# Second half of the tokens in reverse order, so that one product per tile holds the keys of both halves in a gated recurrence

## The chip, the cores and the metric

The kernel runs on one core of a Trainium2 chip. The metric is the device time of one execution in microseconds (us), lower is better. All engines of the core are used: PE (matmuls and weight loads), DVE (elementwise), ACT (activations and copies), POOL, and SP, which issues DMAs.

## The reference, cut to what matters

The reference is one residual block for 256 tokens of width 1024: a SwiGLU FFN, a mixer of two branches (a gated linear recurrence and a forgetting attention), a cross attention to a memory of 256 rows, and a second FFN. The change is in the recurrence (branch A, 8 heads, 128 key channels each) and in what has to follow it. Per head, with a forget gate f between 0 and 1 for each channel:

```
f = lb + (1 - lb) * sigmoid(f_logit);  k = 1 - f;  q = silu(q)
S_t = diag(f_t) S_{t-1} + k_t i_t^T
o_t = S_t^T q_t
```

Written out, token t reads token s <= t with the weight sum over channels of q_t k_s f_{s+1} ... f_t. In the attention (branch B) the logit of t and s has the sum of log f over the tokens after s up to t.

## The kernel before, in words

All work is on 256 tokens, kept as two halves of 128 (index b or h). Every projection is a chain of matmuls on PE: each fp32 weight tile is loaded by SP, copied into a rounded part `hi` on ACT (L126), its rest `lo` is made on DVE (L127), and three products (hi·hi, hi·lo, lo·hi) are added up in PSUM. Three pools set how far loads and copies run ahead: 4 raw tiles, 8 `hi` and 8 `lo` tiles (two chunks of four). Projections write into two PSUM buffers called `mm`; the recurrence writes into four called `acc`.

The recurrence is computed by levels (`LEVELS`, L28, and then 64 and 128; loop at L703). Level 0 is the diagonal s = t. Level m, for m = 1, 2, 4, ..., 128, joins blocks of m tokens in pairs: keys of the earlier block meet queries of the later one. By then each key in an earlier block has been multiplied by all f after it in its block, and each query by all f before it. Heads are taken in two groups of four (`recs`, one `Rec` per group). A level has three steps, each for both groups:

- `products(m)` (L584): matmuls on PE, stationary operand K, moving operand Q, all 128 channels as the contraction. For m below 32 a head and a half are cut into four stretches of 32 tokens, one for each column tile of 32 columns of the array (`tile_position=(0, 32 * k)`). Only half of the 32 keys (the earlier blocks) are of use; the queries are the 16 of the later blocks (`odd`). That is 4 heads x 2 halves x 4 stretches = 32 matmuls a group. An fp32 matmul is two PE instructions, so the trace shows 128 instructions for the two groups of a level. Level 32 has 16 matmuls a group of 32 keys and 32 queries, in two column positions; level 64 has 8, level 128 has 4.
- `grow(m)` (L610): on DVE, Q and K times the products of f of the neighbour block (L619, L620, 512 elements each, two of each a level), and the products of f for blocks twice as large (L624). Both wait until the level's matmuls have read Q and K.
- `keep(m)` (L632): the wanted entries of PSUM go into the matrix AT: for m below 32 by a masked copy on DVE into `ATd` (L636, L638), then by copies on ACT (L641, L643, L646, L649). Each group has a PSUM buffer of its own (`acc`, L587).

PE's order around this is written by hand. `after(i)` (L85) puts a block at high priority behind the i-th matmul of a log; `R_AT` (L45) says behind how many matmuls after `r0` (L652) each level comes. So the levels stand as short bursts between the matmuls of other projections: first the output gate of branch A, three chunks of 344 columns (`gf`, L655, evacuated by L662 on ACT and L663, L665 on DVE), then k_b and q_b of the attention (L689, evacuated by L697). In between come the forget logits of the attention (`forget`, L673): two transposes on PE, then DVE (L678, L679), an Exp and an Ln on ACT (L681, L682), a running sum on DVE (L684) and a DMA out by POOL. Later POOL reads the sums back, spread over all partitions (L731, L735), and masks them (L737). A scheduler orders the other engines' instructions, each engine runs its own in that order.

Of the kernel before, what the change touches and what calls it, by code (L numbers as in the profile page):

```python
# [16 lines left out]
P = 128  # L17
D = 1024
# [49 lines left out]
def block_kernel(ctx: ExitStack, tc: tile.TileContext, wts, head_in, gf_in, x_in, mem_in, memT_in, cols, rows, fbias, masks, out):  # L68
# [134 lines left out]
    masks_s = cp.tile([P, len(LEVELS), 64], I32, name="masks_s")  # L203
# [322 lines left out]

    fT, kT_, qT_ = [], [], []
    for c in range(2):
        u = chunk("f_a", c)
        f, k = m4([P, 4, T], n="f"), m4([P, 4, T], n="k")  # L530
        for j in range(2):
            js = slice(2 * j, 2 * j + 2)
            ps = proj_col2(X2, u, (2 * j, 2 * j + 1))
            f_last = V.tensor_tensor(out=f[:, js], in0=ps, in1=bc(row2, [P, 2, T], 1), op=ALU.mult).ins
            S.activation(f[:, js], f[:, js], AF.Sigmoid)
            for i in (2 * j, 2 * j + 1):
                hd = 4 * c + i
                V.tensor_scalar(out=f[:, i], in0=f[:, i], scalar1=olb[:, hd : hd + 1], scalar2=lbv[:, hd : hd + 1], op0=ALU.mult, op1=ALU.add)
        V.tensor_scalar(out=k, in0=f, scalar1=-1.0, scalar2=1.0, op0=ALU.mult, op1=ALU.add)
        fT.append(f)  # L540
        kT_.append(k)
    for c in range(2):
        u = chunk("q_a", c)
        q = m4([P, 4, T], n="q")
        for j in range(2):
            js = slice(2 * j, 2 * j + 2)
            ps = proj_col2(X2, u, (2 * j, 2 * j + 1))
            z = sp.tile([P, 2, T], F32, tag="z2", name=nm("z2"), bufs=3)
            V.tensor_tensor(out=z, in0=ps, in1=bc(row2, [P, 2, T], 1), op=ALU.mult)
            S.activation(q[:, js], z, AF.Sigmoid)  # L550
            V.tensor_tensor(out=q[:, js], in0=q[:, js], in1=z, op=ALU.mult)
        qT_.append(q)
# [4 lines left out]
    masks32 = cp.tile([P, len(LEVELS) - 1, 32], I32, name="masks32")  # L557
    with tc.issue_after(f_last):
        V.tensor_tensor(out=masks32, in0=masks_s[:, : len(LEVELS) - 1, 0:32], in1=masks_s[:, : len(LEVELS) - 1, 32:64], op=ALU.bitwise_or)

    def odd(a, m):

        return a.rearrange("p (n i m) -> p n i m", i=2, m=m)[:, :, 1] if m else a

    def odd_even(g, m):
        Qv = qT_[g].rearrange("p h t -> p (h t)").rearrange("p (a i m) -> p a i m", i=2, m=m)[:, :, 1]
        Kv = kT_[g].rearrange("p h t -> p (h t)").rearrange("p (a i m) -> p a i m", i=2, m=m)[:, :, 0]
        return Qv, Kv

    class Rec:  # L570


        def __init__(self, g):
            self.g, self.f = g, fT[g]
            self.aux = m4([P, D], n="aux")

            self.ATd = self.aux[:, 256:512]
            self.T = [self.aux[:, 512:], sp.tile([P, T], F32, tag="tq", name=nm("tq"), bufs=2)]
            G.memset(self.ATd, 0.0)
            self.AT = self.f.rearrange("p h t -> p (h t)").rearrange("p (h b t) -> p h b t", h=4, b=2)  # L580
            self.cur = self.f.rearrange("p h t -> p (h t)")
            self.li = 0

        def products(self, m):  # L584

            K, Q = kT_[self.g], qT_[self.g]
            self.ps = acc()  # L587
            if m < 32:
                w = 16 if m else 32
                for i in range(4):  # L590
                    for b in range(2):
                        for k in range(4):
                            t0, o = 128 * b + 32 * k, (i * 2 + b) * w
                            MM(self.ps[32 * k : 32 * k + 32, o : o + w], K[:, i, t0 : t0 + 32], odd(Q[:, i, t0 : t0 + 32], m), start=True, stop=True, tile_position=(0, 32 * k))
            elif m == 32:
                for i in range(4):
                    for b in range(2):
                        for c in range(2):
                            t0, o = 128 * b + 64 * c, (i * 2 + b) * 32
                            MM(self.ps[64 * c : 64 * c + 32, o : o + 32], K[:, i, t0 : t0 + 32], Q[:, i, t0 + 32 : t0 + 64], start=True, stop=True, tile_position=(0, 64 * c))  # L600
            elif m == 64:
                for i in range(4):
                    for b in range(2):
                        t0 = 128 * b
                        MM(self.ps[64 * b : 64 * b + 64, i * 64 : i * 64 + 64], K[:, i, t0 : t0 + 64], Q[:, i, t0 + 64 : t0 + 128], start=True, stop=True)
            else:
                for i in range(4):
                    MM(self.ps[:, i * P : (i + 1) * P], K[:, i, 0:128], Q[:, i, 128:256], start=True, stop=True)

        def grow(self, m):  # L610

            K, Q = kT_[self.g], qT_[self.g]
            if m == 0:
                V.tensor_tensor(out=Q, in0=Q, in1=self.f, op=ALU.mult)
                return
            n = D // (2 * m)
            Tv = self.cur[:, : 2 * n].rearrange("p (a i) -> p a i", i=2)
            Qv, Kv = odd_even(self.g, m)
            V.tensor_tensor(out=Qv, in0=Qv, in1=bc(Tv[:, :, 0], [P, n, m], 2), op=ALU.mult)  # L619
            V.tensor_tensor(out=Kv, in0=Kv, in1=bc(Tv[:, :, 1], [P, n, m], 2), op=ALU.mult)  # L620
            if m < 64:
                nxt = self.T[self.li % 2]
                self.li += 1
                V.tensor_tensor(out=nxt[:, :n], in0=Tv[:, :, 0], in1=Tv[:, :, 1], op=ALU.mult)  # L624
                self.cur = nxt
            if m == 1:

                G.memset(self.AT[64:128, :, :, 0:64], 0.0)
                G.memset(self.AT[32:64, :, :, 0:32], 0.0)
                G.memset(self.AT[96:128, :, :, 64:96], 0.0)  # L630

        def keep(self, m, li):  # L632

            ps, AT = self.ps, self.AT
            if m == 0:
                V.copy_predicated(self.ATd.rearrange("p (a t) -> p a t", t=32), bc(masks32[:, li], [P, 8, 32], 1), ps[:, :256].rearrange("p (a t) -> p a t", t=32))  # L636
            elif m < 32:
                V.copy_predicated(odd(self.ATd, m), bc(odd(masks32[:, li], m), [P, 8, 16 // m, m], 1), ps[:, :128].rearrange("p (n m) -> p n m", m=m))  # L638
            elif m == 32:
                for k in range(4):  # L640
                    S.copy(AT[32 * k : 32 * k + 32, :, :, 32 * k : 32 * k + 32], self.ATd[32 * k : 32 * k + 32].rearrange("p (h b t) -> p h b t", h=4, b=2))  # L641
                for c in range(2):
                    S.copy(AT[64 * c : 64 * c + 32, :, :, 64 * c + 32 : 64 * c + 64], ps[64 * c : 64 * c + 32, :256].rearrange("p (h b t) -> p h b t", h=4, b=2))  # L643
            elif m == 64:
                for b in range(2):
                    S.copy(AT[0:64, :, b, 64:128], ps[64 * b : 64 * b + 64, :256].rearrange("p (h t) -> p h t", h=4))  # L646
            else:
                self.A128 = self.aux[:, 512:].rearrange("p (h t) -> p h t", h=4)
                S.copy(self.A128, ps.rearrange("p (h t) -> p h t", h=4))  # L649
# [23 lines left out]
    def forget(m):  # L673
# [10 lines left out]
        V.tensor_tensor_scan(out=cc, data0=ones[0:8, 0:1].to_broadcast([8, T]), data1=fa, initial=0.0, op0=ALU.mult, op1=ALU.add)  # L684
# [31 lines left out]
    for h in range(2):  # L716
        ps = [acc(), acc()]
        for hd in range(8):
# [3 lines left out]
            MM(o, ATs[g][:, i, h, :], iv[g][:, h, isl], start=True, stop=(h == 0))  # L722
# [10 lines left out]
    for g in range(2):  # L733
        t = m4([P, 4, T], n="cbm")
        G.dma_start(t, cd[4 * g : 4 * g + 4, :].partition_broadcast(P))  # L735
        tv = t.rearrange("p h (b s) -> p (h b) s", b=2)
        G.affine_select(out=tv, in_=tv, pattern=[[0, 8], [-1, P]], compare_op=ALU.is_ge, fill=BIG, base=0, channel_multiplier=1)  # L737
# [283 lines left out]
def _layout(inputs):  # L1021
    import numpy as np

# [39 lines left out]
    def col(v):  # L1063
# [8 lines left out]
    s = np.arange(P)[:, None] % 64  # L1072
    t = np.arange(64)[None, :]
    masks = np.stack(
        [((s == t) if m == 0 else ((s // m) % 2 == 0) & (t // m == s // m + 1)).astype(np.int32) for m in LEVELS], axis=1
    )
    xT = tra(a["x"])
# [5 lines left out]
        "wts": wts[4:], "head": head, "gf": gf, "x": nat(a["x"]), "mem": nat(a["mem"]), "memT": tra(a["mem"]),  # L1083
# [19 lines left out]
```

## Time and profile before

| What | Before |
|---|---|
| median of 3 runs | 801.61 us (801.11 to 801.86) |
| the profiled execution | 801.96 us |
| its span, first to last instruction | 800.2 us |
| granted TensorE clock | 0.999 |
| DVE busy | 521.4 us (65%) |
| ACT busy | 419.1 us (52%) |
| POOL busy | 9.2 us (1%) |

A time of a group in the profile is the sum over its instructions; a time in the chain of waits is the stretch of the span that this piece filled. Matmuls overlap, so the chain tells more of what PE costs than the duration of one matmul. Line numbers are those of the kernel before; all matmuls of projections and products have the line of a helper (L82), so they are told apart by their tiles: `acc<-q,k` are the products of the levels, `mm<-...` are projections.

### The profile page before, as it was taken

To read this page: it belongs to the slowest core of one execution; us is meant where nothing else is said; L and a number is where in the kernel's file an instruction comes from. 1 tells how busy PE (TensorE), PEld (TensorE's weight loads), DVE (VectorE), ACT (ScalarE), POOL (GpSimd) and SP (SyncE) were. 2 spreads that over 40 slices of the span, in tenths; PEclk is the share of its full clock that TensorE was granted. 3 is DMA by queue.
4 is the path that set the end of the run, shared out by engine and by line. 5 is a ranking of instruction groups with operands and counts; after the bars stand their busy time and mean duration, and the time that the engine had idled before them with its cause. 6 is when DMAs were issued, how large, how long until landed. Compare 5 with 4: busy or idle time off the path is not lost.

```text
span 800.2 us, 12839 instructions
## 1 busy us (share of the span) xinstructions
PE 790.6 (99%) x5068; PEld 683.5 (85%) x5068; DVE 521.4 (65%) x824; ACT 419.1 (52%) x636; POOL 9.2 (1%) x21
## 2 busy tenths in 40 slices
PE   9999999999999999999999999999999999999996
PEld 7788888888899999998888888999988888888885
DVE  5774545557767897678675665965749754544543
ACT  6664444546753546447674444754647654434541
POOL 0000000000000100100000000000000000000000
PEclk9999999999999999999999999999999999999999
DMA  8886654564544554643487554455444656554521
GB/s 274 284 272 213 221 197 158 190 205 157 173 169 143 177 188 160 213 169 127 140 300 236 189 177 162 159 187 204 140 152 131 211 193 209 208 204 160 182 81 52
DMA packets 43691, 147.43 MB, mean 184 GB/s; under 512 B 4840, under 2 KB 8304, under 8 KB 43632
## 3 DMA queue, kind: packets, MB, share of 16 engines
q1 hardware_dynamic: 43024, 144.92, 53.0%
q0 software_dynamic: 464, 1.58, 0.6%
q8 instruction: 39, 0.64, 0.3%
q14 instruction: 20, 0.16, 0.1%
q10 hardware_dynamic: 144, 0.13, 0.0%
HBM read 145.56 MB, written 1.06 MB: 183 GB/s over the span
## 4 chain that ended last, share of the span: by engine, by line
PE 95%; DMA 2%; DVE 1%; ACT 1%; issue 0%; SPq 0%; DVEq 0%; ACTq 0%
PE mm L82 67%; PE acc L82 25%; PE tr L349 1%; DMA head<-in_head_dram 1%; PE tr L82 1%; PE tr L269 1%; DMA xs<-in_x_dram 1%; PE tr L783 0%; PE tr L869 0%; PE tr L972 0%; DVE lo L475 0%; ACT junk L232 0%; DVE lT L261 0%; ACT hi L473 0%; DVE lo L127 0%
## 5 line engine op out<-in xcount | busy, mean ns | idle before, releaser
L127 DVE TENSOR_TENSOR lo<-raw,hi 128x1024 fp32r<-128x1024 f32 (+1 forms) x260 | 312.4, 1210 | 127.3 <-ACT hi L126 118.3
L126 ACT CAST hi<-raw 128x1024 fp32r<-128x1024 f32 (+1 forms) x260 | 266.6, 1038 | 160.2 <-PE mm L82 94.9
L82 PE MATMUL mm<-lo,hT 128*128 128x512 f32 (+1 forms) x592 | 227.4, 387 | 0.3 <-DVE lo L127 0.3
L82 PE MATMUL mm<-hi,hT 128*128 128x512 f32 (+1 forms) x592 | 227.4, 386 | 0.0
L82 PE MATMUL mm<-hi,lT 128*128 128x512 f32 (+1 forms) x592 | 226.5, 386 | 0.0
L82 PEld LDWEIGHTS mm<-hi,hT 128*128 128x128 f32 x592 | 111.2, 188 | 22.1 <-ACT hT L260 0.5
L82 PEld LDWEIGHTS mm<-hi,lT 128*128 128x128 f32 x592 | 111.2, 188 | 21.7 <-DVE lT L261 0.5
L82 PEld LDWEIGHTS mm<-lo,hT 128*128 128x128 f32 x592 | 111.1, 188 | 21.1 <-DVE lo L127 0.7
L82 PE MATMUL acc<-hi,act 128*128 128x512 f32 x352 | 112.0, 391 | 0.0
L82 PE MATMUL mm<-hT,hi 128*128 128x256 f32 x384 | 109.2, 284 | 0.0
L82 PE MATMUL mm<-hT,lo 128*128 128x256 f32 x384 | 109.2, 284 | 0.0
L82 PE MATMUL mm<-lT,hi 128*128 128x256 f32 x384 | 109.1, 284 | 0.0
L82 PEld LDWEIGHTS acc<-hi,act 128*128 128x128 f32 x352 | 66.1, 188 | 13.1
L82 PEld LDWEIGHTS mm<-hT,hi 128*128 128x128 f32 x384 | 73.8, 192 | 0.1
L82 PEld LDWEIGHTS mm<-hT,lo 128*128 128x128 f32 x384 | 73.8, 192 | 0.1
L82 PEld LDWEIGHTS mm<-lT,hi 128*128 128x128 f32 x384 | 73.7, 192 | 0.1
L82 PE MATMUL acc<-lo,act 128*128 128x512 f32 x176 | 70.1, 398 | 0.0
L354 ACT ACTIVATE sg<-mm,rstd 128x256 f32<-128x256 f32 x40 | 19.0, 476 | 74.4 <-PE mm L82 74.4
L359 DVE SCALAR_TENSOR_TENSOR at<-mm,rstd,sg 128x256 f32<-128x256 f32 x40 | 19.2, 480 | 56.3 <-ACT sg L354 56.3
L82 PEld LDWEIGHTS acc<-lo,act 128*128 128x128 f32 x176 | 33.1, 188 | 6.2
L82 PE MATMUL acc<-hi,hT 128*128 128x512 f32 x96 | 35.9, 401 | 0.1
L82 PE MATMUL acc<-hi,lT 128*128 128x512 f32 x96 | 35.5, 397 | 0.0
(194 smaller groups left out, 646.3 us busy)
## 6 DMA issues: line engine op xcount, KB each, us to landing
raw<-in_wts_dram SPq DMA_DIRECT2D x248, 512.0 KB, 4.4
raw<-in_gf_dram SPq DMA_DIRECT2D x12, 344.0 KB, 3.9
head<-in_head_dram SPq DMA_DIRECT2D x8, 388.0 KB, 4.0
grow<-in_rows_dram SPq DMA_DIRECT2D x4, 512.0 KB, 5.3
xs<-in_x_dram SPq DMA_DIRECT2D x2, 512.0 KB, 7.6
cbm<-cd POOLq DMA_DIRECT2D x2, 512.0 KB, 9.4
brow<-in_rows_dram SPq DMA_DIRECT2D x4, 256.0 KB, 5.1
memT<-in_memT_dram SPq DMA_DIRECT2D x2, 512.0 KB, 6.7
```

The costliest lines, as they stand in the source:

```text
L82: log.append(PE.matmul(*args, **kw).ins)
L126: S.copy(h, r)
L127: V.tensor_tensor(out=l, in0=r, in1=h.bitcast(F32), op=ALU.subtract)
L269: PE.transpose(ps[:, j * P : (j + 1) * P], src(kb), ident)
L349: PE.transpose(trv[:, j, h * P : (h + 1) * P], ats[c, h][:, j * P : (j + 1) * P], ident)
L354: silu = S.activation(sg, ps[:, :FC], AF.Silu, scale=r2[h])
L359: V.scalar_tensor_tensor(out=a, in0=ps[:, FC:], scalar=r2[h], in1=sg, op0=ALU.mult, op1=ALU.mult)
```

## The change

**The order of the tokens.** The host lays x out with the tokens of the second half in reverse order, and puts the output back. In the recurrence the earlier block of a pair then stands on even places in the first half and on odd places in the second half.

**One product for both halves.** K, Q and f are laid out as half, head, token (`[P, 2, 4, P]`). For levels 1 to 16 a new step `gather` on ACT copies into a tile E the 16 keys in use of a stretch of the first half and the 16 in use of the same stretch of the second half; they fill 32 places with none left over. One matmul with these 32 keys and the 16 + 16 queries of both halves replaces two. Half of its output (keys of one half with queries of the other) isn't used, and the masks leave it out. E uses the two buffers of `brow`, which are used later for the gates' bias.

**Level 32** takes its 16 matmuls a group in four column positions instead of two.

**PSUM.** Both groups share one `acc` buffer in all levels but 128.

**What follows.** `grow` multiplies K ahead of Q. The masks are written out in full, so an operation that combined two sets of them (L559) goes. At level 32 ACT makes 16 copies instead of 12, the added ones smaller. The memsets of AT on POOL are 6 a group instead of 3, of half the size. The running sum of the forget gates is made in two pieces, the second backwards; the mask on POOL is made by half.

The diff, cut to its core:

```diff
+    def by(t, offset, *dims):
+
+        return bass.AP(tensor=t.tensor, offset=t.offset + offset, ap=[list(t.ap[0])] + [list(d) for d in dims if d[1] > 1])
...
+            self.E = sp.tile([P, 512], F32, tag="brow", name=nm("early"), bufs=2)
...
-        def products(self, m):
+        def products(self, m, bank):
...
-                            t0, o = 128 * b + 32 * k, (i * 2 + b) * w
-                            MM(self.ps[32 * k : 32 * k + 32, o : o + w], K[:, i, t0 : t0 + 32], odd(Q[:, i, t0 : t0 + 32], m), start=True, stop=True, tile_position=(0, 32 * k))
+            elif m < 32:
+
+                self.ps = bank[:, self.g * P : self.g * P + P]
+                pv = self.ps.rearrange("p (b h t) -> p b h t", b=2, h=4)
+                for i in range(4):
+                    for k in range(4):
+                        o = i * P + 32 * k
+                        keys = self.E[:, o : o + 32]
+                        queries = by(Q, o + m, (512 - m, 2), (2 * m, 16 // m), (1, m))
+                        MM(pv[32 * k : 32 * k + 32, :, i], keys, queries, start=True, stop=True, tile_position=(0, 32 * k))
             elif m == 32:
...
-                        for c in range(2):
-                            t0, o = 128 * b + 64 * c, (i * 2 + b) * 32
-                            MM(self.ps[64 * c : 64 * c + 32, o : o + 32], K[:, i, t0 : t0 + 32], Q[:, i, t0 + 32 : t0 + 64], start=True, stop=True, tile_position=(0, 64 * c))
+                    for k in range(4):
+                        ks, qs = (slice(32 * j, 32 * j + 32) for j in (k, k ^ 1))
+                        MM(self.ps[ks, i * 32 : i * 32 + 32], K[:, k % 2, i, ks], Q[:, k % 2, i, qs], start=True, stop=True, tile_position=(0, 32 * k))
...
+        def gather(self, m):
+
+            pairs = (2 * m, 256 // m)
+            S.copy(by(self.E, 0, pairs, (m, 2), (1, m)), by(kT_[self.g], 0, pairs, (512 + m, 2), (1, m)))
...
         def grow(self, m):
...
             if m == 0:
+                self.gather(1)
                 V.tensor_tensor(out=Q, in0=Q, in1=self.f, op=ALU.mult)
...
-            V.tensor_tensor(out=Qv, in0=Qv, in1=bc(Tv[:, :, 0], [P, n, m], 2), op=ALU.mult)
-            V.tensor_tensor(out=Kv, in0=Kv, in1=bc(Tv[:, :, 1], [P, n, m], 2), op=ALU.mult)
...
+            times(K, False)
+            if m < 16:
+                self.gather(2 * m)
+            times(Q, True)
...
     for li, m in enumerate(LEVELS + (64, 128)):
         with after(r0 + R_AT[li]):
+            banks = [acc()]
+            banks.append(acc() if m == 128 else banks[0])
             for r in recs:
-                r.products(m)
+                r.products(m, banks[r.g])
```

`times(t, later)` is one multiplication on DVE of the 512 elements of K (earlier blocks) or Q (later blocks) in both halves by the products of f of the neighbour block. `R_AT` and the other offsets of the hand-written order stay as they are.

More of the change, by code (lines that the diff above doesn't have):

```diff
@@ L524, in block_kernel, with heads_of, halves @@
     V.tensor_scalar(out=olb, in0=lbv, scalar1=-1.0, scalar2=1.0, op0=ALU.mult, op1=ALU.add)
+    def heads_of(t, j):
+        return t[:, :, 2 * j : 2 * j + 2].rearrange("p b h t -> p h b t")
+    def halves(ps):
+        return ps.rearrange("p h (b t) -> p h b t", b=2)
+    row2h = row2.rearrange("p (b t) -> p b t", b=2)
     fT, kT_, qT_ = [], [], []
@@ L543, in block_kernel @@
         u = chunk("q_a", c)
-        q = m4([P, 4, T], n="q")
+        q = m4([P, 2, 4, P], n="q")
         for j in range(2):
-            js = slice(2 * j, 2 * j + 2)
+            qj = heads_of(q, j)
             ps = proj_col2(X2, u, (2 * j, 2 * j + 1))
[L548 to L551, printed above, removed]
+            z = sp.tile([P, 2, 2, P], F32, tag="z2", name=nm("z2"), bufs=3)
+            V.tensor_tensor(out=z, in0=halves(ps), in1=bc(row2h, [P, 2, 2, P], 1), op=ALU.mult)
+            S.activation(qj, z, AF.Sigmoid)
+            V.tensor_tensor(out=qj, in0=qj, in1=z, op=ALU.mult)
         qT_.append(q)
[L557 to L568, printed above, removed]
+    def by(t, offset, *dims):
+        return bass.AP(tensor=t.tensor, offset=t.offset + offset, ap=[list(t.ap[0])] + [list(d) for d in dims if d[1] > 1])
     class Rec:
@@ L592, in products @@
                         for k in range(4):
-                            t0, o = 128 * b + 32 * k, (i * 2 + b) * w
-                            MM(self.ps[32 * k : 32 * k + 32, o : o + w], K[:, i, t0 : t0 + 32], odd(Q[:, i, t0 : t0 + 32], m), start=True, stop=True, tile_position=(0, 32 * k))
-            elif m == 32:
+                            o, ks = (b * 4 + i) * 32, slice(32 * k, 32 * k + 32)
+                            MM(self.ps[ks, o : o + 32], K[:, b, i, ks], Q[:, b, i, ks], start=True, stop=True, tile_position=(0, 32 * k))
+            elif m < 32:
[7 more added lines that the diff above has]
+                        MM(pv[32 * k : 32 * k + 32, :, i], keys, queries, start=True, stop=True, tile_position=(0, 32 * k))
+            elif m == 32:
+                self.ps = bank[:, self.g * P : self.g * P + P]
+                for i in range(4):
+                    for k in range(4):
+                        ks, qs = (slice(32 * j, 32 * j + 32) for j in (k, k ^ 1))
+                        MM(self.ps[ks, i * 32 : i * 32 + 32], K[:, k % 2, i, ks], Q[:, k % 2, i, qs], start=True, stop=True, tile_position=(0, 32 * k))
+            elif m == 64:
+                self.ps = bank[:, self.g * 256 : self.g * 256 + 256]
@@ L596, in products @@
                 for i in range(4):
                     for b in range(2):
-                        for c in range(2):
-                            t0, o = 128 * b + 64 * c, (i * 2 + b) * 32
-                            MM(self.ps[64 * c : 64 * c + 32, o : o + 32], K[:, i, t0 : t0 + 32], Q[:, i, t0 + 32 : t0 + 64], start=True, stop=True, tile_position=(0, 64 * c))
-            elif m == 64:
+                        ks, qs = (slice(64 * j, 64 * j + 64) for j in (b, 1 - b))
+                        MM(self.ps[ks, i * 64 : i * 64 + 64], K[:, b, i, ks], Q[:, b, i, qs], start=True, stop=True)
+            else:
+                self.ps = bank
@@ L602, in products @@
                 for i in range(4):
[L603 to L608, printed above, removed]
+                    MM(self.ps[:, i * P : (i + 1) * P], K[:, 0, i], Q[:, 1, i], start=True, stop=True)
@@ L616, in grow, with times @@
             n = D // (2 * m)
-            Tv = self.cur[:, : 2 * n].rearrange("p (a i) -> p a i", i=2)
-            Qv, Kv = odd_even(self.g, m)
-            V.tensor_tensor(out=Qv, in0=Qv, in1=bc(Tv[:, :, 0], [P, n, m], 2), op=ALU.mult)
-            V.tensor_tensor(out=Kv, in0=Kv, in1=bc(Tv[:, :, 1], [P, n, m], 2), op=ALU.mult)
+            def times(t, later):
+                if later:
+                    tv, o, cv = by(t, m, (512 - m, 2), (2 * m, n // 2), (1, m)), 0, n + 1
+                else:
+                    tv, o, cv = by(t, 0, (512 + m, 2), (2 * m, n // 2), (1, m)), 1, n - 1
+                other = bass.AP(tensor=self.cur.tensor, offset=self.cur.offset + o, ap=[list(self.cur.ap[0]), [cv, 2], [2, n // 2]] + ([[0, m]] if m > 1 else []))
+                V.tensor_tensor(out=tv, in0=tv, in1=other, op=ALU.mult)
+            times(K, False)
+            if m < 16:
+                self.gather(2 * m)
+            times(Q, True)
             if m < 64:
+                Tv = self.cur[:, : 2 * n].rearrange("p (a i) -> p a i", i=2)
                 nxt = self.T[self.li % 2]
@@ L626, in grow @@
             if m == 1:
-                G.memset(self.AT[64:128, :, :, 0:64], 0.0)
-                G.memset(self.AT[32:64, :, :, 0:32], 0.0)
-                G.memset(self.AT[96:128, :, :, 64:96], 0.0)
+                for b in range(2):
+                    for k0, q0, w in ((64, 0, 64), (32, 0, 32), (96, 64, 32)):
+                        if b:
+                            k0, q0 = q0, k0
+                        G.memset(self.AT[k0 : k0 + w, b, :, q0 : q0 + w], 0.0)
         def keep(self, m, li):
@@ L683, in forget @@
         V.scalar_tensor_tensor(out=fa, in0=fz, scalar=0.0, in1=fa, op0=ALU.min, op1=ALU.subtract)
-        V.tensor_tensor_scan(out=cc, data0=ones[0:8, 0:1].to_broadcast([8, T]), data1=fa, initial=0.0, op0=ALU.mult, op1=ALU.add)
+        for h in range(2):
+            cv, fv = (t[:, h * P : (h + 1) * P] for t in (cc, fa))
+            if h:
+                cv, fv = cv[:, ::-1], fv[:, ::-1]
+            V.tensor_tensor_scan(out=cv, data0=ones[0:8, 0:1].to_broadcast([8, P]), data1=fv, initial=cc[:, P - 1 : P] if h else 0.0, op0=ALU.mult, op1=ALU.add)
         G.dma_start(cd, cc)
@@ L721, in block_kernel @@
             o = ps[g][:, isl]
-            MM(o, ATs[g][:, i, h, :], iv[g][:, h, isl], start=True, stop=(h == 0))
+            MM(o, ATs[g][:, h, i, :], iv[g][:, h, isl], start=True, stop=(h == 0))
             if h == 1:
@@ L735, in block_kernel @@
         G.dma_start(t, cd[4 * g : 4 * g + 4, :].partition_broadcast(P))
-        tv = t.rearrange("p h (b s) -> p (h b) s", b=2)
-        G.affine_select(out=tv, in_=tv, pattern=[[0, 8], [-1, P]], compare_op=ALU.is_ge, fill=BIG, base=0, channel_multiplier=1)
+        for b, sign in ((0, 1), (1, -1)):
+            tv = t[:, :, b * P : (b + 1) * P]
+            G.affine_select(out=tv, in_=tv, pattern=[[0, 4], [-sign, P]], compare_op=ALU.is_ge, fill=BIG, base=0, channel_multiplier=sign)
         cbm.append(t)
@@ L1071, in _layout @@
     rows = np.stack([a[n][0] for n in ("ffn1_post_g", "mix_post_g", "mem_post_g", "ffn2_post_g")] + list(a["b_gate"][0].reshape(2, D)))
[L1072 to L1077, printed above, removed]
+    s = np.arange(P)[:, None] % 32
+    t = np.arange(32)[None, :]
+    masks = [s == t]
+    for m in LEVELS[1:6]:
+        for b in range(2):
+            later = (t // m == s // m + 1) if b == 0 else (t // m == s // m - 1)
+            ok = ((s // m) % 2 == b) & later
+            masks += [ok[:, (t[0] // m) % 2 == 1 - b]] * 4
+    masks = np.concatenate(masks, axis=1).astype(np.int32)
+    x = np.concatenate([a["x"][:, :P], a["x"][:, : P - 1 : -1]], axis=1)
+    xT = tra(x)
     gain = col(a["ffn1_pre_g"][0])
```

49 lines of the change are left out of this document (29 added, 20 removed).

## The prediction, made before the changed kernel was run

> **What bounds the kernel now.** I read the page first (busy shares and shares of the chain of waits), then the waits of PE.
>
> ```profile
> span 800.2 us, 12839 instructions
> PE 790.6 (99%) x5068; PEld 683.5 (85%) x5068; DVE 521.4 (65%) x824; ACT 419.1 (52%) x636; POOL 9.2 (1%) x21
> PE 95%; DMA 2%; DVE 1%; ACT 1%; issue 0%; SPq 0%; DVEq 0%; ACTq 0%
> ```
>
> ```profile
> PE tr L82 <- DVE ones L195: 1.1, 1, 1.1
> PE acc L82 <- issue: 1.0, 1, 1.0
> PE mm L82 <- DVE lo L127: 0.3, 1, 0.3
> ```
>
> PE fills 95% of the chain that ended last, and it waits for other engines for 1.4 us in all (1.1 + 0.3). So PE's order of work sets the time: a microsecond taken from PE in the middle comes out at the end, as long as the other engines keep ahead. What has to be known is how long the bursts of the levels are on PE. The chain in order of time, over the levels, shows it (start, length, what; the count is of the records that the chain met, not of all):
>
> ```profile
> 265.89 1.37 PE acc L82 x85
> 267.26 5.57 PE mm L82 x34
> 272.83 1.23 PE acc L82 x88
> 274.05 5.56 PE mm L82 x34
> 279.61 1.49 PE acc L82 x102
> 281.10 5.57 PE mm L82 x34
> 286.66 1.22 PE acc L82 x84
> 287.89 5.91 PE mm L82 x40
> 293.79 1.09 PE acc L82 x76
> 294.88 0.97 issue
> 295.85 0.32 PE acc L82 x15
> ...
> 302.06 1.23 PE acc L82 x83
> ...
> 309.00 1.14 PE acc L82 x64
> ...
> 315.84 1.08 PE acc L82 x32
> ```
>
> Each piece `acc` is the burst of one level, in the order 0, 1, 2, 4, 8, 16, 32, 64; the pieces `mm` between them are projections. Level 8 stands in three rows, since 0.97 us in it are a pause in which PE waited for nothing that the trace names. The shapes behind them:
>
> ```profile
> L82 PE MATMUL acc<-q,k 128*32 128x16 f32 x640 | 6.9, 185 | 1.0 <-issue 1.0
> ...
> L82 PE MATMUL acc<-q,k 128*32 128x32 f32 x192 | 2.6, 199 | 0.0
> ...
> L82 PE MATMUL acc<-q,k 128*64 128x64 f32 x32 | 1.2, 225 | 0.0
> ```
>
> 640 instructions with 16 queries are the five levels 1 to 16, 128 each; 192 with 32 queries are level 0 (128) and level 32 (64); the 32 with 64 queries are level 64.
>
> **The change part by part.** *Levels 1 to 16 on PE.* They take 1.23 + 1.49 + 1.22 + (1.09 + 0.97 + 0.32) + 1.23 = 7.55 us now. After the change each has 64 instructions of 32 keys and 32 queries instead of 128 of 32 and 16. No row has just that. Level 0 has the same shape in four column tiles, 128 of them in 1.37 us, so half is 0.69. Level 32 has 64 of them in 1.14, but in two column positions. The lower bound is half of a burst with 16 queries, 0.62; the upper is 1.14. The nearest row is level 0's; with 0.06 us for the ends of a burst, which do not halve (an estimate), I take 0.75. Five bursts then take 3.75, and 3.80 us go.
>
> Of these, some 1.2 are the pauses (0.97 in level 8, and 1.49 − 1.22 = 0.27 in level 2). I take them as gone, for they stand only in bursts that run 128 instructions within 1.2 us, and there will be 64.
>
> ```profile
> 280.25:295.85 15.60, 14.63 (x383) 14.07 (x383) 15.50 (x29) 8.69 (x10) 0.00 (x0) 1.00 0.53 176
> ```
>
> ```profile
> q8 instruction: 39, 0.64, 0.3%
> ```
>
> From the pause in level 2 (280.25) to the end of that in level 8 (295.85) PE ran 383 matmuls (the view by windows; first PE, weight loads, DVE, ACT), with their weight loads 766 instructions, and the page's queue q8 moved 39 packets of 0.64 MB together, 16 KB each. [...] That the pauses stay is a rival below.
>
> *Level 32 on PE.* 64 instructions in four column positions: 1.14 becomes 0.75 by the same reckoning (bounds 0.62 and 1.14), 0.39 us go. Levels 0, 64 and 128 keep count and shape: nothing.
>
> *DVE.* `grow` keeps its multiplications, 512 elements each; Q and K are strided now too. But DVE is full in this stretch: 15.50 of 15.60 us in the row above. What can be late when PE is faster is the evacuation that frees a PSUM buffer of the projections:
>
> ```profile
> 290.71 0.55 DVE L663 SCALAR_TENSOR_TENSOR G<-mm,rstd,z 128x336 f32<-128x336 f32 x1
> 291.18 0.20 DVE L665 TENSOR_SCALAR zf<-mm,rstd 128x8 f32<-128x8 f32 x1
> ```
>
> ```profile
> 291.55 0.34 PE L82 MATMUL mm<-hT,hi 128*128 128x256 f32 x1
> ```
>
> The first k_b matmul (291.55) writes the buffer that DVE releases at 291.38, 0.17 us earlier. Levels 1, 2 and 4 shorten PE's way there by 0.48 + 0.74 + 0.47 = 1.69. If DVE keeps its order it starts earlier only by what level 1 gives (0.48), and PE waits 1.69 − 0.17 − 0.48 = 1.04. If the scheduler puts the evacuation ahead of the two weight splits that stand before it, PE waits for nothing:
>
> ```profile
> 285.36 2.34 DVE L127 TENSOR_TENSOR lo<-raw,hi 128x1024 fp32r<-128x1024 f32 x2
> ```
>
> These splits are of k_b's weights, whose first use is at 291.55, so they can stand back; and K's products no longer wait for the burst of their level, since the burst reads E. Bounds 0 and 1.04; neither is nearer, and I take 0.5 back. Behind a late start of k_b nothing else queues: the evacuation after it follows PE.
>
> *ACT.* Ten gathers of 128x512 are added, and at level 32 eight copies of 32x128 take the place of four of 32x256.
>
> ```profile
> L649 ACT COPY aux<-acc 128x512 f32<-128x512 f32 x2 | 1.2, 586 | 0.7 <-PE acc L82 0.7
> ```
>
> ```profile
> L643 ACT COPY f<-acc 32x256 f32<-32x256 f32 x4 | 1.4, 361 | 0.0
> ```
>
> At 0.59 each the gathers are 5.9 us, spread over some 40 us; ACT is busy 8.69 of 15.60 us in the stretch where DVE is full, and projections hide them. Twice the duration (source elements 2 KB apart) still fits: a level's two gathers then take 2.4 us against 5.56 between bursts. A gather adds two waits: for the burst that read the old E and for K's product on DVE. Queued behind it on ACT are weight copies (L126) and the sigmoid of an output gate (L662); weight splits lead their use by 3.85 us and more (the two above end at 287.70, k_b begins at 291.55), which is the cover. If it went, the PE burst would wait for a gather, at most 1.2 us a level. The eight small copies cost at most 8 x 0.36 instead of 4 x 0.36, 1.4 us of ACT, before weight copies with the same lead: nothing.
>
> *The rest.* The mask by half doubles the count of this:
>
> ```profile
> L737 POOL TENSOR_SCALAR_AFFINE_SELECT cbm<-cbm 128x1024 f32<-128x1024 f32 x2 | 2.2, 1090 | 8.8 <-DMA cbm<-cd 8.8
> ```
>
> At most 2.2 us more on POOL for the masks (if size were free), at least nothing. POOL is at 1%, and PE's only waits are the three rows at the top, none of them for POOL: nothing. The memsets run there too. The running sum is one short DVE operation more, on 8 partitions, in a stretch in which DVE idles. The mask DMA grows by half, once, in the first FFN, where PE hardly waits. One DVE operation (L559) goes.
>
> *The sum.* −3.80 − 0.39 + 0.5 = −3.7 us. The profiled execution took 801.96, so 798.3; the median shown is 0.35 lower, which gives **797.9**.
>
> **The rivals.** *The pauses stay* or move to another burst: 1.2 us come back, gain 2.5, 799.1. For it: nothing that I see sets them but the position in the stream, which shifts. Against it: the four other bursts of 128 ran without one.
>
> *DVE takes PE's place as the bound* between 280 and 296. PE loses 0.47 + 1.63 = 2.1 us there, DVE has 0.1 to give; 2.0 of the 4.2 come back (in place of the 0.5): gain 2.2, 799.4. For it: the 15.50. Against it: much of that work is splits with a lead.
>
> *A gather stands behind the Exp.*
>
> ```profile
> 301.42 0.42 ACT L681 ACTIVATE fa<-fa 8x256 f32<-8x256 f32 x1 [6.59 <-DVE fa L679]
> 301.85 1.28 ACT L682 ACT_TABLE_LOAD   x1
> 303.15 0.42 ACT L682 ACTIVATE fa<-fa 8x256 f32<-8x256 f32 x1
> ```
>
> ACT's queue stood 6.59 us before the Exp of the forget gates. If level 16's two gathers were put behind it and the Ln, they would end at 303.57 + 1.2 = 304.8, 2.7 us after the start of level 16 (302.06); the Exp's operand waits for DVE work that PE's own k_b sets, so this distance stays when PE is faster. Gain 3.7 − 2.7 = 1.0, 800.6. Against it: DVE makes the products of K that the gathers need before the operand of the Exp.
>
> *Slower: the new bursts do not overlap their column tiles.* Those of levels 1 to 16 write their output in two runs of 16, no burst now does. If an instruction then took what level 64's take, (1.08 − 0.12)/32 = 30 ns (0.12 for the ends, an estimate), a burst would take 64 x 30 ns + 0.12 = 2.04, the five 10.20 against 7.55 now; less the 0.39 of level 32, whose output stays in one run, that is 2.3 us slower, 803.9. It turns slower above 7.94/5 = 1.59 a burst, 23 ns an instruction; level 0 shows about 11. Against it: Q was read in strides by the levels 1 to 16 at one speed (1.22 or 1.23, without pauses), runs of 1 as of 16. [...]
>
> **How the numbers follow.** The forecast has 0.58, the pauses 0.13, DVE 0.12, the Exp 0.09, the slower one 0.08. The range: with all bursts at their lower bound, 7.55 − 3.1 + 0.52 = 4.97 us go and no wait comes, 796.6; at the upper bound of 1.14, 7.55 − 5.7 = 1.85 go less 0.5, 1.35, 800.3. This takes in the first three cases, 0.83. A measurement of this kernel tells about 0.2% from no change, 1.6 us. Faster by more: forecast, pauses and most of DVE, 0.80; within: the Exp and the rest of DVE, 0.11; slower 0.09.
>
> **What would show it.** Bursts of levels 1 to 32 of about 0.75 us in the chain, with no row "issue" among them; a wait of PE for DVE at the first k_b matmul of 0 to 1 us; no wait of PE for ACT at a level; later pieces of the chain as long as before. Bursts of 1.2 or more, or a wait at each level, would make the prediction wrong.

## The result and the profile after

| What | Before | After |
|---|---|---|
| median of 6 runs | 801.56 us (801.11 to 802.20) | 797.94 us (797.19 to 798.41) |
| ratio, 95% interval | | 0.9952 (0.9942 to 0.9962) |
| the profiled execution | 801.96 us | 798.41 us |
| its span | 800.2 us | 796.6 us |

The forecast was 797.9. The engines' line of the page after the change:

```profile
PE 787.1 (99%) x4748; PEld 679.3 (85%) x4748; DVE 519.8 (65%) x824; ACT 426.6 (54%) x650; POOL 11.7 (1%) x29
```

PE has 320 matmuls less (5068 to 4748) and as many weight loads less; its busy time fell by 3.5 us, the span by 3.6. Line numbers are those of the changed kernel from here on: its helper for matmuls is L84, the forget logits' evacuation L709 (before L665), the transposes of them L721 (before L677). The waits of PE:

```profile
PE tr L84 <- DVE ones L197: 1.1, 1, 1.1
PE mm L84 <- DVE lo L129: 0.7, 1, 0.7
PE tr L721 <- DVE zf L709: 0.5, 1, 0.5
```

The row `acc <- issue` of 1.0 is gone: no pause is left. A wait that wasn't there has come, at the transposes of the forget logits. The chain of waits over the levels (start, length, what):

```profile
273.11 0.69 PE acc L84 x57
273.80 5.57 PE mm L84 x34
279.37 0.69 PE acc L84 x54
...
299.63 0.69 PE acc L84 x50
300.33 5.70 PE mm L84 x46
306.03 0.69 PE acc L84 x50
```

Levels 1, 2, 16 and 32 are 0.69 each. Levels 4 and 8 lie in the part left out, where the chain leaves PE for the new wait. In PE's timeline, where level 1 is 0.77 and level 16 is 0.76, both are bursts like the others (start, length from the first start to the last end, what):

```profile
285.56 0.76 PE L84 MATMUL acc<-q,early 128*32 128x32 f32 x64
...
292.36 0.76 PE L84 MATMUL acc<-q,early 128*32 128x32 f32 x64
```

So six bursts of 0.69, 4.14 us, stand where 8.69 stood before (7.55 and level 32's 1.14): 4.55 us less. The stretch as a whole, by the windows from the start of level 0 to the start of level 128, of the kernel before and then of the changed one (window, its length, busy PE, weight loads, DVE, ACT, POOL):

```profile
265.82:322.47 56.65, 55.68 (x1194) 53.92 (x1194) 49.84 (x87) 30.64 (x46) 3.90 (x8) 1.00 0.53 178
```

```profile
266.12:319.05 52.93, 52.44 (x873) 50.42 (x873) 47.13 (x86) 34.61 (x56) 3.81 (x14) 1.00 0.52 170
```

3.72 us went there. The start of level 0 came 0.30 later and what follows level 128 took 0.18 less, which makes the 3.6 of the span. 4.55 less 3.72 leaves 0.83 that was given back inside the stretch. PE's timeline shows where:

```profile
289.67 0.32 PE L84 MATMUL mm<-lo,hT 128*128 128x344 f32 x1
289.83 0.32 PE L84 MATMUL mm<-hi,lT 128*128 128x344 f32 x1
290.18 0.36 PE L84 MATMUL mm<-hT,hi 128*128 128x256 f32 x1
290.37 0.28 PE L84 MATMUL mm<-lT,hi 128*128 128x256 f32 x1
290.49 0.28 PE L84 MATMUL mm<-hT,lo 128*128 128x256 f32 x1
...
296.12 0.28 PE L84 MATMUL mm<-hT,lo 128*128 128x256 f32 x1
296.86 0.27 PE L721 MATMUL tr<-ident,zf 128*8 128x128 f32 x1 [0.46 <-DVE zf L709]
```

The gate's matmuls of 344 columns start 0.16 apart (289.67, 289.83), and before the change the first of k_b started 0.16 after the last of them as well (291.40 to 291.55). Now it starts 0.35 after (290.18), 0.19 too late. Matmuls of k_b start 0.12 apart (290.37, 290.49). The transpose starts 0.74 after the one ahead of it (296.12 to 296.86), 0.62 too late. Together 0.81.

Both waits are for DVE's evacuations of the forget logits, the first at k_b (in the first row below it ends at 290.02, 0.16 before the first k_b matmul; before the change the distance was 0.17). Why the transpose waits is in DVE's order, after the change:

```profile
289.81 0.21 DVE L709 TENSOR_SCALAR zf<-mm,rstd 128x8 f32<-128x8 f32 x1
...
293.09 0.57 DVE L707 SCALAR_TENSOR_TENSOR G<-mm,rstd,z 128x336 f32<-128x336 f32 x1 [0.79 <-ACT z L706]
...
296.58 0.22 DVE L709 TENSOR_SCALAR zf<-mm,rstd 128x8 f32<-128x8 f32 x1
```

and before it:

```profile
293.10 0.22 DVE L665 TENSOR_SCALAR zf<-mm,rstd 128x8 f32<-128x8 f32 x1
...
295.50 0.68 DVE L619 TENSOR_TENSOR q<-q,aux 128x512 f32<-128x512 f32 x1
```

Before, the second evacuation of the forget logits stood ahead of level 8's `grow`. Now the scheduler has put it behind the whole of level 8 (`grow` and `keep`, in the rows left out from 293.57 to 296.58), and that work itself starts late, because G waited 0.79 us for the sigmoid on ACT. The sigmoid stood behind a weight copy that waited for its load:

```profile
291.57 1.05 ACT L128 CAST hi<-raw 128x1024 fp32r<-128x1024 f32 x1 [1.64 <-DMA raw<-in_wts_dram]
292.53 0.53 ACT L706 ACTIVATE z<-mm,rstd 128x336 f32<-128x336 f32 x1
```

An evacuation of 0.22 us that nobody seemed to be short of thus had the 3.0 us of level 8 put ahead of it. Why the scheduler changed the order isn't known.

### The profile page after: what moved, and what is told of

It is laid out like the page before. It is cut to its first block, busy times and chain, and to the rows that moved or that the text cites. A ratio compares the mean times of both kernels' runs of the same rounds, so it can differ in the third digit from the quotient of the medians.

```text
span 796.6 us, 12213 instructions
## 1 busy us (share of the span) xinstructions
PE 787.1 (99%) x4748; PEld 679.3 (85%) x4748; DVE 519.8 (65%) x824; ACT 426.6 (54%) x650; POOL 11.7 (1%) x29
## 3 DMA queue, kind: packets, MB, share of 16 engines
HBM read 145.67 MB, written 1.06 MB: 184 GB/s over the span
## 4 chain that ended last, share of the span: by engine, by line
PE 94%; DMA 3%; DVE 2%; ACT 1%; issue 0%; SPq 0%; DVEq 0%; ACTq 0%
PE mm L84 66%; PE acc L84 24%; PE tr L351 1%; DMA head<-in_head_dram 1%; PE tr L84 1%; DMA xs<-in_x_dram 1%; PE tr L271 1%; DMA raw<-in_wts_dram 1%; PE tr L834 0%; PE tr L920 0%; PE tr L1023 0%; ACT junk L234 0%; DVE lo L477 0%; DVE lT L263 0%; ACT hi L475 0%
## 5 line engine op out<-in xcount | busy, mean ns | idle before, releaser
L84 PE MATMUL mm<-lo,hT 128*128 128x512 f32 (+1 forms) x592 | 227.2, 386 | 0.7 <-DVE lo L129 0.7
L84 PE MATMUL mm<-hi,hT 128*128 128x512 f32 (+1 forms) x592 | 227.1, 386 | 0.1
L84 PE MATMUL mm<-hi,lT 128*128 128x512 f32 (+1 forms) x592 | 226.1, 385 | 0.0
L84 PEld LDWEIGHTS mm<-hi,hT 128*128 128x128 f32 x592 | 111.1, 188 | 22.4 <-ACT hT L262 0.6
L84 PEld LDWEIGHTS mm<-hi,lT 128*128 128x128 f32 x592 | 111.1, 188 | 21.7 <-DVE lT L263 0.5
L84 PEld LDWEIGHTS mm<-lo,hT 128*128 128x128 f32 x592 | 111.0, 188 | 21.5 <-DVE lo L129 1.1
L84 PE MATMUL acc<-hi,act 128*128 128x512 f32 x352 | 111.9, 390 | 0.0
L84 PE MATMUL mm<-hT,hi 128*128 128x256 f32 x384 | 109.1, 284 | 0.0
L84 PE MATMUL mm<-hT,lo 128*128 128x256 f32 x384 | 109.0, 284 | 0.0
L84 PE MATMUL mm<-lT,hi 128*128 128x256 f32 x384 | 108.9, 284 | 0.0
L84 PEld LDWEIGHTS acc<-hi,act 128*128 128x128 f32 x352 | 66.1, 188 | 13.1
L84 PEld LDWEIGHTS mm<-hT,hi 128*128 128x128 f32 x384 | 73.6, 192 | 0.4 <-PE mm L84 0.3
L84 PEld LDWEIGHTS mm<-hT,lo 128*128 128x128 f32 x384 | 73.6, 192 | 0.1
L84 PEld LDWEIGHTS mm<-lT,hi 128*128 128x128 f32 x384 | 73.6, 192 | 0.1
L84 PE MATMUL acc<-lo,act 128*128 128x512 f32 x176 | 70.0, 398 | 0.0
L84 PEld LDWEIGHTS acc<-lo,act 128*128 128x128 f32 x176 | 33.1, 188 | 6.2
L84 PE MATMUL acc<-hi,hT 128*128 128x512 f32 x96 | 35.8, 401 | 0.1
L84 PE MATMUL acc<-hi,lT 128*128 128x512 f32 x96 | 35.2, 394 | 0.0
```

What stands on the lines that cost most here:

```text
L84: log.append(PE.matmul(*args, **kw).ins)
```

## The experiments

The theory: the gain is the time of fewer instructions in the bursts, 0.69 for each of six, with the pauses gone because the bursts are half as dense; what is given back is DVE's place for the forget logits' evacuations. The rivals: the gain is from something else (the layout, the start, level 32's order); the pauses went because they moved; ACT's gathers, not DVE, give the time back.

**Do the products of levels 1 to 16 carry the gain?** In the changed kernel these products are issued twice, so that PE has as many instructions as before.

```diff
-                for i in range(4):
+                for i in [0, 1, 2, 3] * 2:
```

> The changed kernel with every product of levels 1 to 16 issued twice (the second writes the same values), so that a level has 128 instructions again and all else is as in the changed kernel. Theory (the gain is PE's instruction count in the bursts): each of the five bursts goes from 0.69 back to about 1.27 us, so +2.9 us, about 800.8, and up to 1.2 more if pauses come back in them. Rival (the gain comes from what else changed: shared PSUM buffers, the gathered keys that let DVE start on K earlier, one DVE operation less): stays within 0.5 us of 797.9.

Measured: 800.79 us (12 runs) beside 801.71, ratio 0.9986 (0.9977 to 0.9995). The chain over levels 1 to 32:

```profile
272.88 1.25 PE acc L84 x88
...
293.89 1.12 PE acc L84 x75
295.01 0.24 issue
295.25 0.33 PE acc L84 x15
...
308.48 0.69 PE acc L84 x51
```

With the number of instructions back, the bursts are as long as before (1.25 for level 1, 1.25 to 1.30 for levels 2, 4 and 16 in the rows left out) and most of the gain is gone, although the layout, the gathers, the masks and level 32 stay changed. Level 32, not doubled, keeps its 0.69. From level 0 to level 128 this kernel takes 55.60 us, 1.05 less than before: level 32 is 0.45 shorter, levels 2 and 8 with their pauses 0.88, levels 1, 4 and 16 are 0.11 longer, and the first k_b matmul is 0.16 late. That is 1.06, and leaves nothing for the rest of the change. A pause is back too, in level 8, ahead of the last 15 of its 128 matmuls, as before; but it is 0.24, not 0.97. There is no wait at the forget logits in this chain: PE is later and DVE keeps ahead.

**What do column tiles in turn bring at level 32?** Three orders of the same 64 instructions of the changed kernel's level 32, whose order is to take four column tiles in turn: two tiles in turn, neighbours (0 and 1, then 2 and 3); two tiles in turn with one between (0 and 2, then 1 and 3); one tile at a time.

```diff
-                for i in range(4):
-                    for k in range(4):
+                for i, k in [(i, k0 + j) for k0 in (0, 2) for i in range(4) for j in range(2)]:
+                    if True:
```

> The changed kernel with level 32's 64 instructions issued in an order that uses two column tiles in turn, then the two others, instead of four in turn. Theory (bursts are limited by each column tile, four in turn overlap best): the burst of level 32 goes from 0.69 back to about 1.1 us, +0.4 us, about 798.3. Rival (only the number of instructions counts): the burst stays at 0.69, no difference.

```diff
-                for i in range(4):
-                    for k in range(4):
+                for i, k in [(i, k0 + j) for k0 in (0, 1) for i in range(4) for j in (0, 2)]:
+                    if True:
```

> The changed kernel with level 32's instructions in an order that uses column tiles 0 and 2 in turn and then 1 and 3, as far apart as in the kernel before, where the burst took 1.14 us; with tiles 0 and 1 in turn and then 2 and 3 it took 0.87. Theory (the distance of the two tiles matters): about 1.1 us. Rival (the kernel before was slower for another reason, such as keys and queries of one head in one layout): 0.87 again. Total within noise of 797.9.

```diff
-                for i in range(4):
-                    for k in range(4):
+                for k in range(4):
+                    for i in range(4):
```

> The changed kernel with level 32's instructions in an order that stays in one column tile for 16 instructions at a time. Theory (an instruction waits for the one before it in its own column tile, so tiles in turn overlap): about 2 us for the burst of level 32, as at 30 ns an instruction, against 0.69 with four in turn. Rival (only the number of instructions counts): 0.69 to 0.87.

Measured: 797.93 us, ratio 0.9948 (0.9934 to 0.9962), for the first; one run each of the others, 797.92 and 798.43. The burst of level 32 in PE's timeline, for the changed kernel, two neighbours in turn (with one tile between, it is 0.94 as well) and one tile at a time:

```profile
305.96 0.76 PE L84 MATMUL acc<-q,k 128*32 128x32 f32 x64
```

```profile
305.26 0.94 PE L84 MATMUL acc<-q,k 128*32 128x32 f32 x64
```

```profile
305.14 1.51 PE L84 MATMUL acc<-q,k 128*32 128x32 f32 x64
```

A record lasts about 0.20, so from the first start to the last it is 0.56, 0.74, 0.74 and 1.31 us for 63 steps: 9, 12, 12 and 21 ns an instruction with four, two, two and one tile in turn. How far apart the two tiles lie doesn't matter. In the chain the bursts are 0.69, 0.87, 0.87 and 1.44 us: neither the 1.1 expected for two tiles nor the 2 expected for one came, so tiles in turn overlap, and fewer tiles cost less than expected. Before, level 32 with two column positions took 1.21 in PE's timeline, 16 ns a step; two tiles in turn now take 12. That difference (before, the positions were 64 columns apart and a tile's place was given as `64 * c`) wasn't resolved. The time of the whole kernel doesn't tell the orders apart: they differ by less than the 1.2 us over which the runs of the changed kernel spread.

**Are the pauses tied to a place in the stream of instructions?** Two variants of the kernel before: `WARM`, the number of matmuls on ones at the very start, raised from 8 to 18 and cut to 4. Each of them is two PE matmul records, so all later ones stand 20 places further on, or 8 places earlier; the levels are untouched.

```diff
-WARM = 8
+WARM = 18
```

> The kernel before with 10 more matmuls on constants at the very start, 20 more pairs of PE instructions, which moves all later instructions 20 pairs along the stream. Theory (the pauses stand where a block of 256 PE instructions ends and the next is not there yet): the 0.97 us pause leaves the 114th matmul of level 8; if one is there it is at the 94th, or it stands in another level 20 earlier than a block's end before. Rival (something in level 8 itself makes PE wait): about 1 us at the 114th matmul again. Cost at the start 0 to 3 us, since PE waits there for its first data anyway.

```diff
-WARM = 8
+WARM = 4
```

> The kernel before with 4 matmuls on constants less at the very start, 8 pairs of PE instructions fewer, which moves the ends of instruction blocks 8 pairs later among the levels. Theory (pauses stand at the ends of blocks of 256 PE instructions): the pause in level 8, after 113 of its 128 matmul records before, stands after 121 of them, again of about 1 us. Rival (the pause belongs to something that level 8 does, or comes by chance): after 113 again, or none. Total within 1.5 us of before.

Measured with 18: 802.87 us, ratio 1.0014 (1.0005 to 1.0023). No burst has a pause; the chain:

```profile
268.53 1.38 PE acc L82 x85
...
282.25 1.25 PE acc L82 x100
...
296.46 1.23 PE acc L82 x85
```

Level 2 (282.25) has 1.25 and level 8 (296.46) 1.23 where 1.49 and 2.38 stood. The time is longer all the same, for level 0 starts 2.6 us later (268.53 for 265.89): the longer start costs more than the pauses had. Measured with 4: 801.42 us, ratio 0.9999 (0.9989 to 1.0008). PE's timeline in level 8:

```profile
293.87 1.23 PE L82 MATMUL acc<-q,k 128*32 128x16 f32 x121
295.29 0.25 PE L82 MATMUL acc<-q,k 128*32 128x16 f32 x7 [0.20 <-issue]
```

The pause stands behind 121 matmuls of the level, where it stood behind 113 before: 8 places on, at the same place of the whole stream. So the place is tied to the stream of instructions, not to a level or a time. The size isn't: 0.97, 0.24 (with doubled products), 0.20, and with 18 nothing at all, where the same place lies behind 93 matmuls of level 8. With 4 a pause of about 1 us was expected, and it was 0.20. Level 2 has no pause with 18 or with 4; PE then comes early to k_b, and the first matmul there is 0.24 and 0.23 late in the old layout too.

The times of the packets of queue q8 (`instruction`) in the traces tell what sets the size. It moved 39 packets of 16 KB before and 37 after, about one for every 128 matmuls with their weight loads (5068 and 4748 matmuls). Between the two pauses of the kernel before, three landed (at 283.08, 289.77 and 294.38) while PE ran 383 matmuls and as many weight loads, 766 instructions: 255 a packet, beside the 256 in what was expected. Each of the four pauses seen (levels 2 and 8 before, level 8 with 4 and with doubled products) ends 1.34 to 1.48 us after such a packet has landed: in level 8 before at 295.85, 1.47 after 294.38; with 4 at 295.29, 1.34 after 293.95. Counted from the pauses there is such a place every 128 matmuls, so one in each burst of levels 1 to 16 before. In all twelve profiles every place but those four is passed 1.96 us or more after the landing, without a pause; with 18, PE comes to the place in level 8 some 3.9 us after. In the changed kernel two of the places lie in bursts, those of levels 4 and 8, and PE passes them 8.4 and 3.4 us after the landing. Between levels 1 and 16 it takes PE at least 7.0 us there from one place to the next; before, the place ahead of level 8's pause and that pause were 2.9 us of work apart (291.85 to 294.70). So the pauses did not just move out of the bursts: the sparser bursts give the packets time to land. A burst of 128 need not pause either, as 18 shows.

**Do the gathers cost anything?** Each gather of the changed kernel is done twice, ten copies more on ACT.

```diff
-            S.copy(by(self.E, 0, pairs, (m, 2), (1, m)), by(kT_[self.g], 0, pairs, (512 + m, 2), (1, m)))
+            for _ in range(2):
+                S.copy(by(self.E, 0, pairs, (m, 2), (1, m)), by(kT_[self.g], 0, pairs, (512 + m, 2), (1, m)))
```

> The changed kernel with every gather done twice (the second writes the same values): ten more copies of 0.6 us on ACT, 6 us. Theory (projections hide the gathers, and a level's gathers end long before its burst): no PE wait for ACT at a level, within 0.5 us of 797.9. Rival (ACT has become the next bound, so the gathers already cost something): up to 1.2 us a level, 2 to 6 us more, with PE waits for the gathered tile.

Measured: 797.66 us, ratio 0.9951 (0.9934 to 0.9967). The view of the tile E (count, shortest, median and longest in ns, first and last start):

```profile
L630 ACT COPY early<-k x20: 611/618/865, 234.2 to 294.7; 128x512 f32<-128x512 f32 x20
```

Twenty copies of 0.62 instead of ten, some 6 us more of ACT, and the time doesn't rise. The gathers are hidden. They aren't what delays the sigmoid either: with twice as many, the transpose starts 0.59 after the matmul ahead of it, for 0.74. The chain of the changed kernel does name a gather ahead of the load that held the sigmoid up, but that load was issued at 286.40, before the gather ended (286.71) and right after DVE's weight splits did (286.35).

**Is DVE's queue what gives time back?** The evacuation of the forget logits moves from DVE to ACT.

```diff
-                V.tensor_scalar(out=zf[h], in0=ps[:, n:GF], scalar1=r2[h], scalar2=None, op0=ALU.mult)
+                S.activation(zf[h], ps[:, n:GF], AF.Copy, scale=r2[h])
```

> The changed kernel with the forget logits' evacuation (128x8, twice) on ACT instead of DVE. Theory (what is left of waits is DVE's queue: the transposes of the forget logits wait 0.62 us and the first k_b matmul 0.23 us): both go, -0.6 to -0.85 us, about 797.2. Rival (PE would wait there for something else, such as PSUM buffers or the gate's own evacuation): the wait stays or moves, within 0.2 us of 797.9.

Measured: 797.48 us (796.69 to 799.21), ratio 0.9948 (0.9935 to 0.9960). The chain where PE waited:

```profile
289.21 0.28 ACT zf L709
289.48 0.04 issue
289.53 2.30 PE mm L84 x17
...
292.52 1.87 PE mm L84 x14
294.39 0.22 PE tr L721 x2
```

The wait at the transposes is gone: they follow the projection without a gap. The first matmul of k_b (289.53) still waits, by 0.26, now for the evacuation on ACT; both waits had been expected to go. In its profile the stretch from level 0 to level 128 is 52.45 us (265.40 to 317.85) for 52.93, 0.48 of the 0.62. In the median of the whole the 0.5 is within the spread of the runs.

**A version without both waits.** The evacuation on ACT as above, and levels 4 to 64 eight matmuls further back in PE's order of work, beside the changed kernel once more on the same chip.

```diff
-R_AT = (18, 52, 86, 120, 160, 206, 252, 298, 344)
+R_AT = (18, 52, 86, 128, 168, 214, 260, 306, 344)
```

> The changed kernel with the forget logits' evacuation on ACT and with levels 4 to 64 placed 8 matmuls later among the projections, so that DVE evacuates the output gate ahead of level 4's multiplications. Theory (the two waits left are DVE's queue): both waits go, 0.5 to 0.85 us faster than the changed kernel beside it. Rival (the waits move to a later level, since the time from level 64 to 128 gets 8 matmuls shorter): no difference.

> The changed kernel once more, beside the next run on one chip. 797.9 us, and a wait of PE of 0.2 to 0.7 us for DVE at the transposes of the forget logits and of 0.2 to 0.4 at the first k_b matmul.

Measured: 796.79 us (796.63 to 797.08), ratio to before 0.9939 (0.9926 to 0.9951); the changed kernel as it is 798.08 (797.34 to 798.33), ratio 0.9950 (0.9937 to 0.9964). PE's waits in its profile are the first two rows of those shown for the changed kernel (1.1 and 0.7), both ahead of level 0, and no third. The changed kernel beside it has both waits again, 0.45 at the transposes and 0.19 at k_b. From level 0 to level 128 it takes 52.08 us (265.29 to 317.37) where the changed kernel beside it took 52.79 (266.16 to 318.95): 0.71 of the 1.29 lie in this stretch, where the two waits were. The rest lies at the start, where the edit changes nothing; level 0 began between 265.3 and 266.3 in all kernels with this first part, so 0.6 of it isn't claimed.

## Why the prediction was right, point by point

- **PE bounds the kernel, and what PE loses comes out at the end:** held. 4.55 us less in the bursts, 0.81 given back, 3.72 in the stretch, 3.6 in the span. That the bursts carry it is shown by doubling them.
- **Bursts of 0.75:** a size that was off. They take 0.69. The row that it was taken from is too long: level 0's piece is 1.37, but 128 instructions of its shape take 1.25, in level 1 with doubled products and in level 0 itself with `WARM` at 4. Half of 1.25 and the 0.06 for the ends make 0.69. Why level 0 takes 0.1 more in the other kernels isn't known. Six times 0.06 is 0.36 us, so 4.55 went where 4.19 was expected.
- **The 1.2 us of pauses go:** held. The bursts have 64 instructions, as the prediction counted, and what that brings is time for the packets: where level 8's pause stood, PE needed 2.9 us from one place to the next, and in the changed kernel, between levels 1 and 16, it needs 7.0 or more. The position in the stream, which the prediction has under the rival that the pauses stay, is borne out by the 8 places. The 39 and 37 packets agree: there is one for 260 and for 257 of PE's instructions (5068 and 4748 matmuls with as many weight loads). What the prediction did not say is that most of these places cost nothing, in the kernel before too: the pause depends on when the packet landed, 1.34 to 1.48 us before the end of each of the four, and with 1.96 us or more there was none.
- **The 0.5 us for DVE's queue:** the step that failed, in size and place. The first k_b matmul lost 0.19, within the bounds of 0 and 1.04. But "Behind a late start of k_b nothing else queues: the evacuation after it follows PE" was wrong: the second evacuation of the forget logits was put behind all of level 8, and the transposes that read it stand in PE's own queue, where they cost 0.62. 0.81 came back in place of 0.5.
- The two misses, +0.36 and −0.31, nearly cancel, and the runs of the changed kernel spread over 1.2 us. Apart from the step at DVE the mechanism was right; that the forecast met the median to 0.04 us was luck.
- **ACT's gathers cost nothing:** held, at 0.61 to 0.86 us each, 0.62 in the median (0.59 was taken), and at twice their number too. No PE wait for them came.
- **The masks on POOL:** the upper bound, and hidden. Four masks of half the size take 4.2 us, where two took 2.2:

```profile
L788 POOL TENSOR_SCALAR_AFFINE_SELECT cbm<-cbm 128x512 f32<-128x512 f32 x4 | 4.2, 1082 | 7.9 <-DMA cbm<-cd 7.9
```

- **The rivals:** the pauses did not stay; the Exp of the forget gates had no gather behind it that PE waited for. DVE did become a bound for 0.81 us, less than half of the 2.0 that this rival priced. The slower one, that an output in two runs keeps column tiles from overlapping, fell: 0.69 in levels 1 to 16 (two runs of 16) and 0.69 in level 32 (one run).

## What to carry to other kernels

Where small matmuls ran densely over column tiles here, their number set the time (1.32 us for 128 with 32 queries, 0.76 for 64) and the queries in each hardly did (1.30 for 128 with 16), so filling half-empty stationary tiles paid even with half of the output thrown away. Before counting the gain, look for small operations on a full engine that feed the bound engine's own queue: a scheduler may put much work ahead of them once the bound engine is faster, 3.0 us ahead of one of 0.22 here. Copies on an engine that is half idle (ACT, busy 54%, ten of 0.62 us) can pay for it, as long as a projection lies between them and their use (5.57 us here).

## What the runs showed of the hardware

- **Output in two runs cost nothing.** With 128 instructions of 32 keys and 32 queries, level 0 in the variant with `WARM` at 4 (output in one run) and level 1 with doubled products (two runs of 16) take the same time:

```profile
266.06 1.32 PE L82 MATMUL acc<-q,k 128*32 128x32 f32 x128
```

```profile
272.81 1.32 PE L84 MATMUL acc<-q,early 128*32 128x32 f32 x128
```

In every other kernel level 0 takes 1.43 to 1.45 by this view, with its output in one run as well.

- **Twice the queries cost next to nothing:** 1.32 here against 1.30 for 128 instructions with 16 queries (level 16 of the kernel before, start at 302.00).
- **Column tiles in turn:** 9 ns an instruction with four, 12 with two, 21 with one.
- **A mask on POOL of half the size takes as long:** 1082 ns for 128x512 and 1090 for 128x1024.
- **After a pause PE went on about 1.4 us behind the landing of an instruction packet:** 1.34 to 1.48 in the four pauses seen; wherever in the twelve profiles the packet had landed 1.96 us or more ahead, there was none.
